# A decoder layer on one core: large raw tiles for the MLP's chained weights, one copy per value tile, and a later place for two steps of the attention's end

## The chip, the cores and the metric

The kernel runs on one core of a Trainium2 chip. The time is device microseconds of one execution; what counts is the median over runs.

## The reference, cut to what matters

One layer of a hybrid decoder over 512 tokens of width 1024, all in float32:

```
h = RMSNorm(x);  z = h @ W_in            # 1024 x 9728: retention q,k,v,gate; three attention groups q,k,v; two merge gates
A = retention(q, k, v), four heads, group RMSNorm, times swish(gate)
B = three groups of dilated causal window attention, (window, dilation) = (128,1), (512,4), (2048,16),
    QK-norm and rotary, the groups merged by their softmax denominators
x = x + W_o( sig(g_A) * (A @ W_A) + sig(g_B) * (B @ W_B) )
x = x + W_down( relu(RMSNorm(x) @ W_up)^2 )          # 4096 wide
x = x + sig(RMSNorm(x) @ W_pg) * (p @ W_pp)
```

## The kernel before, in words

**Matmuls in three parts.** Each float32 operand is split into a high part (rounded to the fast format, ACT, L250) and a low part (what is left, DVE, L251); a product is three matmuls, high x high, high x low, low x high (`mm3`, L262 to L264).

**Seven products instead of eight.** Most large products are done by `seven_products` (L1249): a 2 x 2 block scheme with seven products 1 to 7, each of two halves over the contraction. Its weights are seven blocks: B11, B21, B22 as they are, and T1 to T4, which are sums. A *unit* is half of such a block, 256 x 512 numbers. `SEVEN` and `HALVES` (L34, L37) are two orders of the products: `SEVEN` begins with halves (1,0), (5,0), (1,1), (5,1), `HALVES` with (1,0), (1,1), (5,0), (5,1); the rest is the same. Product 1 uses B11 and product 5 uses T1, so the units' order at the start is B11.0, T1.0, B11.1, T1.1 in `SEVEN` and B11.0, B11.1, T1.0, T1.1 in `HALVES`.

**The plan of weights.** `make_plan` (L1457) lists all units in the order of use; `plan_seven` (L171) makes the units of one seven. T2 grows out of T1's raw tile, T3 out of B22's and T4 out of T2's: when a unit is split, an accumulating DMA on the POOL queue adds another block onto the same raw tile (L228). So T1's and B22's raw tiles stay in use until the split of T4 and T3. A block named in `vector` gets its sum on DVE instead (L226, T1 += B11, T4 = T2 + B21): `self.added` says behind which unit's split it is put into the program.

**Buffers.** Raw tiles come from a ring of 6 (`wraw`, L87; 4 KB in each partition), the split ones from rings of 4, activations from 16 large buffers of 8 KB (`bigp`, L89): in the MLP seven for the normed input, two for the residual, up to seven for the inner activation `U`. `fetch` (L199) puts loads on SP's queue (L212); `ahead` (L217) splits units up to 2 ahead of their use.

**Order of the work.** `later` (L110) hangs a step on a clock that ticks with every half product of one side (6 matmuls); `tick` (L122) releases due steps. Three stretches, among them the first projection and the last down product, keep the program's order on ACT and DVE (`manual_schedule`); elsewhere the framework's scheduler orders each engine's instructions.

**Around the change.** `attention` (L699) does the projections of the three groups, their scores and values. `values_seven` (L732) makes the values of a group as a seven and, for the second half of its output, writes each of four value tiles in dilated order, token 4l + q to row l, place q: four DMAs each, one per q (L763, L764), on SP. `scores` (L771) hangs a block's softmax on the clock, and `turn` (L802) hangs the transposes of its exponentials on PE (L694) 5, 8 or 11 ticks behind it, by group. For the last group, `rescale` (L856) first merges the denominators (L863 to L878), scales the exponentials on ACT (L876) and transposes the merged factors on PE (L884). Behind it come the projection for the rotated queries (`ret_cols`, L992), and `retention` (L1013) with two pairs of heads, each with a seven for values and gates (L1045, planned at L1468). The MLP in `tail` (L1408) has four rounds of an up and a down product, 256 columns a matmul in up and 512 in down, planned at L1474 and L1475. The seven of the last group's values is called S2 below.

Of the kernel before, what the change touches and what calls it, by code (L numbers as in the profile page):

```python
# [11 lines left out]
F32 = mybir.dt.float32  # L12
# [5 lines left out]
P = 128  # L18
# [9 lines left out]
DIL = 4  # L28
# [51 lines left out]
class Block:  # L80


    def __init__(self, ctx, tc, a):
# [18 lines left out]
        self.hook = None  # L102
        self.chained, self.added = {}, {}
        self.spare = False
        self.plan, self.raws, self.loaded, self.used = [], [], [], 0
# [64 lines left out]

    def plan_seven(self, w, r0, c1, c2, order, vector=()):  # L171

# [5 lines left out]
        for name, u in units:  # L178
            if name == "T1":
                src = q(0, 1, u) if name in vector else (q(0, 1, u), q(0, 0, u))  # L180
                if name in vector:
                    self.added[at("B11", u)] = at("T1", u), at("B11", u)
            elif name == "T4" and name in vector:
                self.added[max(at("B21", u), at("T2", u))] = at("T2", u), at("B21", u)
                src = (None, at("T2", u))
            elif name[0] == "B":
                src = q(int(name[1]) - 1, int(name[2]) - 1, u)
            else:
                prev, ij = {"T2": ("T1", (1, 1)), "T3": ("B22", (0, 1)), "T4": ("T2", (1, 0))}[name]
                k = at(prev, u)  # L190
                self.chained[k] = q(*ij, u)
                src = (None, k)
            self.plan.append((src, None))

# [4 lines left out]
    def fetch(self, n):  # L199
        while len(self.raws) < min(len(self.plan), n):  # L200
# [4 lines left out]
            if src is None:  # L205
                self.raws.append((self.raws[add[0]][0], None))
                continue
            raw = self.wraw.tile([P, 1024], F32, tag="raw", name=self.nm("raw"))
            k = src.shape[0] // P
# [522 lines left out]
    def values_seven(self, scale, ready=None):  # L732
# [11 lines left out]
        def after(m, p, ps):  # L744
# [17 lines left out]
            if m in (6, 7):  # L762
                for q in range(DIL):  # L763
                    nc.sync.dma_start(tile(1)[32 * t : 32 * (t + 1), q], o[q : P : DIL])  # L764
            if m in (2, 4) and ready is not None:
# [5 lines left out]
    def scores(self, g, qT, kT, rq, past, held=None, lag=2):  # L771
# [7 lines left out]
        def block(r):  # L779
# [19 lines left out]
            for e in es:  # L799
                self.later((5, 8, 11)[g], lambda e=e: turn(e, r), ("pT", g, r))  # L800

# [211 lines left out]
    def retention(self, dec, kd):  # L1013
# [8 lines left out]
        for pr in range(2):  # L1022
# [21 lines left out]

            self.seven_products(left, after)  # L1045
            A.append(self.big("A"))
# [410 lines left out]
    def make_plan(self):  # L1457
# [9 lines left out]
        for c in (0, 512):  # L1467
            self.plan_seven(w, 0, RV + c, RG + c, SEVEN, ("T1", "T4"))  # L1468
        self.plan_mix()
# [3 lines left out]
        for f in range(NF // 2):  # L1473
            self.plan_seven(a["w_up"][0], 0, 1024 * f + 512, 1024 * f, HALVES, ("T1",))  # L1474
            self.plan_seven(a["w_down"][0], 1024 * f, 512, 0, HALVES, ("T1",))  # L1475
        for half in range(2):
# [40 lines left out]
```

## Time and profile before

| | |
|---|---|
| median of 3 runs | 952.26 us (951.79 to 953.13) |
| the profiled execution's own time | 955.36 us |
| its span, first to last instruction | 953.6 us |
| mean granted TensorE clock | 0.997 |
| share of the span: PE, DVE, ACT, POOL | 99%, 75%, 59%, 17% |
| MLP, four rounds | 585 to 895 us of the span |

PE is the matmul engine; PEld its loading of the stationary operand, which overlaps; DVE, ACT, POOL and SP are the vector, scalar, GpSimd and sync engines, and a q behind a name is an engine's queue of instructions. The granted clock is the share of full speed that the matmul engine gets. A wait in brackets is the idle time of the engine just before the instruction, with what ended it; where several things were waited for, the profile names the last. Matmul records overlap: at full clock, one of 512 columns starts every 0.23 us, though its record is 0.39 us long.

### The profile page before, as it was taken

Reading aid. Unit: us, or ns where it says so; the run is one execution under the profiler, and the core shown is the slowest. Engines: PE = TensorE matmul, PEld = TensorE weight load, DVE = VectorE, ACT = ScalarE, POOL = GpSimd, SP = SyncE. Lnnn points to the kernel's source line nnn. Section 1 sums busy time; section 2 is a strip of 40 time slices with the busy share of each in tenths; the row PEclk is TensorE's granted clock in tenths of the full one; section 3 lists DMA queues with packets and bytes.
Section 4 is the critical chain, followed back from the end, with each engine's and each line's share of the span. In section 5 each row is a group of like instructions: output and inputs, shape, how many; then the busy total and the mean of one; then the engine's idle time right before and its main releaser. Section 6 shows DMA issues by size and latency. Waiting matters only on the chain.

```text
span 953.6 us, 14325 instructions
## 1 busy us (share of the span) xinstructions
PE 943.3 (99%) x5357; PEld 826.2 (87%) x5357; DVE 718.4 (75%) x997; ACT 562.1 (59%) x1065; POOL 159.5 (17%) x140
## 2 busy tenths in 40 slices
PE   9999999999899999999999999999999999999998
PEld 6888888888788888999988888988998998998887
DVE  7789964766697849386937889799499689769953
ACT  5657775445745566576714446884494486467651
POOL 0322210222001112223012211111212302112100
PEclk9999999999999999999999999999999999999999
DMA  9953466258437645869737677868958968876911
GB/s 333 282 170 82 106 141 215 64 118 195 148 111 155 173 100 138 163 181 217 232 115 236 148 178 214 206 153 222 199 156 202 191 183 157 224 172 159 288 50 56
DMA packets 92549, 162.87 MB, mean 171 GB/s; under 512 B 8608, under 2 KB 20544, under 8 KB 92480
## 3 DMA queue, kind: packets, MB, share of 16 engines
q1 hardware_dynamic: 65168, 113.37, 36.4%
q0 software_dynamic: 23936, 46.14, 29.0%
q10 hardware_dynamic: 3376, 2.44, 0.9%
q8 instruction: 42, 0.69, 0.3%
q14 instruction: 27, 0.22, 0.1%
HBM read 153.49 MB, written 6.34 MB: 168 GB/s over the span
## 4 chain that ended last, share of the span: by engine, by line
PE 92%; DVE 3%; ACT 1%; issue 1%; DMA 1%; POOL 1%; SPq 0%; ACTq 0%; POOLq 0%; DVEq 0%
PE pg L264 25%; PE pg L262 25%; PE pg L263 25%; PE pa L264 3%; PE pa L263 3%; PE pa L262 3%; PE po L835 1%; PE ph L590 1%; DVE wlo L251 1%; PE pe L694 1%; PE sc L787 1%; PE ry L1083 1%; PE kv L1070 1%; PE ry L1085 1%; DVE ro L578 0%
## 5 line engine op out<-in xcount | busy, mean ns | idle before, releaser
L251 DVE TENSOR_TENSOR wlo<-raw,whi 128x1024 fp32r<-128x1024 f32 (+1 forms) x258 | 306.8, 1198 | 112.7 <-ACT whi L250 111.8
L250 ACT ACTIVATE whi<-raw 128x1024 fp32r<-128x1024 f32 (+1 forms) x257 | 266.3, 1041 | 212.1 <-PE pg L264 87.2
L263 PE MATMUL pg<-f,whi 128*128 128x256 f32 x384 | 108.7, 283 | 0.0
L264 PE MATMUL pg<-f,wlo 128*128 128x256 f32 x384 | 108.7, 283 | 0.0
L262 PE MATMUL pg<-f,whi 128*128 128x256 f32 x384 | 108.7, 283 | 0.0
L262 PE MATMUL pg<-whi,hh 128*128 128x512 f32 x248 | 98.6, 398 | 0.0
L264 PE MATMUL pg<-whi,hl 128*128 128x512 f32 x248 | 97.1, 392 | 0.0
L263 PE MATMUL pg<-wlo,hh 128*128 128x512 f32 x248 | 96.8, 390 | 0.0
L262 PE MATMUL pg<-whi,f 128*128 128x512 f32 x192 | 75.4, 393 | 0.0
L263 PE MATMUL pg<-wlo,f 128*128 128x512 f32 x192 | 74.8, 389 | 0.0
L264 PE MATMUL pg<-whi,f 128*128 128x512 f32 x192 | 74.8, 389 | 0.0
L262 PEld LDWEIGHTS pg<-f,whi 128*128 128x128 f32 x384 | 73.7, 192 | 0.2
L263 PEld LDWEIGHTS pg<-f,whi 128*128 128x128 f32 x384 | 73.7, 192 | 0.2
L264 PEld LDWEIGHTS pg<-f,wlo 128*128 128x128 f32 x384 | 73.7, 192 | 0.0
L228 POOL DMA_DIRECT2D raw<-in_w_in x32 | 38.9, 1216 | 197.8 <-DVE wlo L251 193.0
L264 PEld LDWEIGHTS pg<-whi,hl 128*128 128x128 f32 x248 | 46.6, 188 | 9.8
L263 PEld LDWEIGHTS pg<-wlo,hh 128*128 128x128 f32 x248 | 46.6, 188 | 9.2
L262 PEld LDWEIGHTS pg<-whi,hh 128*128 128x128 f32 x248 | 46.6, 188 | 9.2
L228 POOL DMA_DIRECT2D raw<-in_w_down x24 | 29.0, 1215 | 139.3 <-DVE wlo L251 108.2
L262 PE MATMUL pg<-whi,us 128*128 128x512 f32 x128 | 52.1, 407 | 0.0
L228 POOL DMA_DIRECT2D raw<-in_w_up x24 | 29.0, 1211 | 135.0 <-DVE wlo L251 124.7
L264 PE MATMUL pg<-whi,us 128*128 128x512 f32 x128 | 50.0, 391 | 0.0
(280 smaller groups left out, 2298.0 us busy)
## 6 DMA issues: line engine op xcount, KB each, us to landing
raw<-in_w_in SPq DMA_DIRECT2D x72, 512.0 KB, 4.1
raw<-in_w_in POOLq DMA_DIRECT2D x32, 512.0 KB, 6.2
raw<-in_w_up SPq DMA_DIRECT2D x32, 512.0 KB, 4.6
raw<-in_w_down SPq DMA_DIRECT2D x32, 512.0 KB, 4.6
raw<-in_w_up POOLq DMA_DIRECT2D x24, 512.0 KB, 6.6
raw<-in_w_down POOLq DMA_DIRECT2D x24, 512.0 KB, 5.9
x<-in_x SPq DMA_DIRECT2D x8, 512.0 KB, 8.2
raw<-in_w_ret_out SPq DMA_DIRECT2D x8, 512.0 KB, 3.8
```

The costliest lines, as they stand in the source:

```text
L228: self.nc.gpsimd.dma_start(raw, self.chained[i].rearrange("(k p) n -> p k n", p=P), accum_op=ALU.add)
L250: self.pin(nc.scalar.activation(R(hi[:, i]), raw[:, i], AF.Copy))
L251: nc.vector.tensor_tensor(R(lo[:, i]), raw[:, i], hi[:, i], op=ALU.subtract)
L262: t.matmul(ps, sh, mh, start=first, stop=False, skip_group_check=more)
L263: t.matmul(ps, sh, ml, start=False, stop=False, skip_group_check=more)
L264: t.matmul(ps, sl, mh, start=False, stop=last, skip_group_check=more)
L590: self.nc.tensor.transpose(ps[:, t * P : (t + 1) * P], rots[t][:, h * HD : (h + 1) * HD], self.ident)
L694: self.nc.tensor.transpose(ps[:, k * P : (k + 1) * P], e[:, k * P : (k + 1) * P], self.ident)
L787: nc.tensor.matmul(sc[:, h * P : (h + 1) * P], qT[:, h, rs], kT[:, h, rs], start=True, stop=True)
L835: nc.tensor.matmul(po[:, h * P : (h + 1) * P], v[:, vt, h * HD : (h + 1) * HD], pt, start=b == 0, stop=b == len(blocks) - 1)
L1070: nc.tensor.matmul(ps, kd[:, n, hs], v[:, n, c], start=True, stop=True)
L1083: nc.tensor.matmul(y, sT[0][:, r], v[:, i, c], start=True, stop=i == 0)
```

## The change

Four edits:

- T1's and B22's raw tiles of the MLP's products come from the large buffers, one for both halves.
- A value tile is written in dilated order by one DMA.
- The retention's two sevens are planned and run in `HALVES`, and where T4 is summed on DVE too, the sum T1 += B11 is put one unit later into the program: half 0 behind the split of B11.1, half 1 behind the split of T1.0.
- The last group's exponentials are transposed 15 ticks behind their softmax instead of 11.

```diff
-    def plan_seven(self, w, r0, c1, c2, order, vector=()):
+    def plan_seven(self, w, r0, c1, c2, order, vector=(), wide=()):
...
                 if name in vector:
-                    self.added[at("B11", u)] = at("T1", u), at("B11", u)
+                    self.added[at("B11", u) if "T4" not in vector else at("T1", u) - 1] = at("T1", u), at("B11", u)
...
+            if name in wide:
+                self.wide[len(self.plan)] = at(name, 0), u
             self.plan.append((src, None))
...
     def fetch(self, n):
...
-            raw = self.wraw.tile([P, 1024], F32, tag="raw", name=self.nm("raw"))
+            if len(self.raws) in self.wide:
+                n, u = self.wide[len(self.raws)]
+                if n not in self.pairs:
+                    self.pairs[n] = self.big("raw")
+                raw = self.pairs[n][:, 2 * u : 2 * u + 2].rearrange("p a b -> p (a b)")
+            else:
+                raw = self.wraw.tile([P, 1024], F32, tag="raw", name=self.nm("raw"))
...
             if m in (6, 7):
-                for q in range(DIL):
-                    nc.sync.dma_start(tile(1)[32 * t : 32 * (t + 1), q], o[q : P : DIL])
+                nc.sync.dma_start(tile(1)[32 * t : 32 * (t + 1)], o)
...
-                self.later((5, 8, 11)[g], lambda e=e: turn(e, r), ("pT", g, r))
+                self.later((5, 8, 15)[g], lambda e=e: turn(e, r), ("pT", g, r))
...
-            self.seven_products(left, after)
+            self.seven_products(left, after, HALVES)
...
-            self.plan_seven(w, 0, RV + c, RG + c, SEVEN, ("T1", "T4"))
+            self.plan_seven(w, 0, RV + c, RG + c, HALVES, ("T1", "T4"))
...
-            self.plan_seven(a["w_up"][0], 0, 1024 * f + 512, 1024 * f, HALVES, ("T1",))
-            self.plan_seven(a["w_down"][0], 1024 * f, 512, 0, HALVES, ("T1",))
+            self.plan_seven(a["w_up"][0], 0, 1024 * f + 512, 1024 * f, HALVES, ("T1",), ("T1", "B22"))
+            self.plan_seven(a["w_down"][0], 1024 * f, 512, 0, HALVES, ("T1",), ("T1", "B22"))
```

More of the change, by code (lines that the diff above doesn't have):

```diff
@@ L103, in __init__ @@
         self.chained, self.added = {}, {}
+        self.wide, self.pairs = {}, {}
         self.spare = False
```

## The prediction, made before the change was run

> **What bounds the kernel now.** I read the page first, then the waits of TensorE, then the timeline around the one long wait, then tables by stretch.
>
> ```profile
> span 953.6 us, 14325 instructions
> PE 943.3 (99%) x5357; PEld 826.2 (87%) x5357; DVE 718.4 (75%) x997; ACT 562.1 (59%) x1065; POOL 159.5 (17%) x140
> ```
>
> TensorE is busy for 943.3 of 953.6 us, and the change neither adds nor removes a matmul. So nothing is to be won but the 10.3 us in which PE waits, and what hides in slow matmuls. The waits of PE alone (who waited for whom: us in total, times, longest) are a short list:
>
> ```profile
> PE pc L884 <- DVE wide L878: 3.0, 1, 3.0
> PE warm L439 <- DVE warm L435: 1.4, 1, 1.4
> PE sc L795 <- DVE sm L678: 0.8, 1, 0.8
> PE pg L493 <- ACT hh L473: 0.3, 1, 0.3
> PE pg L262 <- ACT pp L533: 0.2, 1, 0.2
> ```
>
> Two of the five lie at the start (L439, L493), one in the first attention group (L795), one in the embedding (L533); the diff touches none of them. One is left: the transpose at L884 in `rescale(2)`, which waits 3.0 us for `wide`. The timeline of all engines (start, us, engine, line, what; idle before it in brackets) shows why:
>
> ```profile
> 247.70 1.23 DVE L251 TENSOR_TENSOR wlo<-raw,whi 128x1024 fp32r<-128x1024 f32 x1 [0.27 <-ACT whi L250]
> ...
> 249.64 1.22 DVE L251 TENSOR_TENSOR wlo<-raw,whi 128x1024 fp32r<-128x1024 f32 x1
> ...
> 251.69 0.20 ACT L864 ACTIVATE f<-f 128x16 f32<-128x16 f32 x1
> ...
> 252.48 0.39 PE L262 MATMUL pg<-whi,hh 128*128 128x512 f32 x1
> 252.70 0.39 PE L263 MATMUL pg<-wlo,hh 128*128 128x512 f32 x1
> 253.73 1.22 DVE L226 TENSOR_TENSOR raw<-raw,raw 128x1024 f32<-128x1024 f32 x1 [2.79 <-DMA v<-m]
> 254.22 1.04 SPq L212 DMA_DIRECT2D raw<-in_w_in  x2
> 254.88 0.17 DVE L866 TENSOR_TENSOR w<-f,st 128x16 f32<-128x16 f32 x1
> ...
> 255.63 4.79 ACT L876 ACTIVATE se<-se,inv 128x128 f32<-128x128 f32 x16 [2.86 <-DVE inv L870]
> 255.78 0.18 DVE L878 COPY wide<-f 128x16 f32<-128x16 f32 x1
> 256.11 0.37 PE L884 MATMUL pc<-ident,wide 128*16 128x128 f32 x1 [3.02 <-DVE wide L878]
> 256.13 0.78 PE L264 MATMUL pg<-whi,hl 128*128 128x512 f32 x1
> 256.71 0.63 PE L694 MATMUL pe<-ident,se 128*128 128x128 f32 x2
> ```
>
> The small steps that make `wide` (L866 to L878) could start when ACT is done with L864, at 251.69 + 0.20 = 251.89. But ahead of them in DVE's queue stands L226, the sum T1 += B11 for the first retention pair, which waits 2.79 us for a transfer. The profile names the value copies; the queue says which transfer it was:
>
> ```profile
> 244.40 1.58 SPq L212 DMA_DIRECT2D raw<-in_w_in  x2
> 246.87 7.26 SPq L764 DMA_DIRECT2D v<-m  x8
> ```
>
> The second of the two loads started at 245.6 us. Asked for line L212 in the stretch 245.5 to 246.0, the trace gives its time to landing:
>
> ```profile
> DMA to landing us min/median/max: 8.0/8.0/8.0
> ```
>
> For all L212 loads of the program the same row reads:
>
> ```profile
> DMA to landing us min/median/max: 3.3/4.4/10.9
> ```
>
> 245.6 + 8.0 = 253.6, and the sum starts at 253.73. So a weight load that took 8.0 instead of 4.4 us held DVE, DVE held `wide`, and `wide` held PE. The wait has a tail (columns: PE, PEld, DVE, ACT, POOL busy, then granted clock, DMA share, GB/s):
>
> ```profile
> 105.00:110.00 5.00, 4.17 (x20) 3.25 (x19) 5.00 (x8) 2.25 (x6) 1.24 (x1) 1.00 0.16 15
> ...
> 256.00:258.00 2.00, 1.89 (x8) 1.56 (x8) 0.00 (x0) 2.00 (x9) 0.00 (x0) 0.50 0.93 352
> 258.00:260.00 2.00, 2.00 (x10) 1.53 (x10) 0.00 (x0) 2.00 (x8) 0.00 (x0) 0.67 0.35 135
> 260.00:265.00 5.00, 5.00 (x27) 4.15 (x26) 4.26 (x8) 4.88 (x13) 0.00 (x0) 1.00 0.27 87
> ```
>
> After the 3.02 us the granted clock is 0.50 for 2 us and 0.67 for 2 us: 2 x 0.50 + 2 x 0.33 = 1.66 us more. The shorter wait of 0.8 us near 108 left it at 1.00. The whole place costs 3.02 + 1.66 = 4.7 us.
>
> **The change, part by part.** *Sums a unit later, product one's halves first.* The order of the pair becomes B11.0, B11.1, T1.0, T1.1 instead of B11.0, T1.0, B11.1, T1.1. The load that started at 244.40 stays B11.0, but the one at 245.6 becomes B11.1, on which no early sum depends. T1.0 is now the third load, one of the pair that went out at 254.22. The two splits at 247.70 and 249.64 free raw buffers at 248.9 and 250.9, so it can go out at about 249 at the earliest and lands at 249 + 4.4 = 253.4 by the median. If the sum then stands behind the small steps, these run from 251.89 to 251.89 + (255.78 + 0.18 - 254.88) = 252.97, and L884, which followed `wide` by 0.15 us, goes at 253.12. PE would reach it 0.23 us (252.48 to 252.70) after its last matmul, at 252.93. Of 3.02 us 0.2 is left, and the low clock goes: 4.5 us gained. What is late next there is ACT: its 16 scalings (4.79 us) then run from about 252.4 to 257.2, beside matmuls.
>
> *Last exponentials later.* The 16 transposes of `e` (L694) stand right behind L884 on PE, and each needs one of the 16 scalings. Unmoved and without the wait, they would begin near 253.5 and wait for ACT until about 257: up to 3.5 us given back. Four ticks are 4 x 6 matmuls x 0.23 = 5.5 us, so they come at about 259, after the scalings. The cover is the rotation's projection (`ret_cols`), whose matmuls need none of this. The reader behind them is the weighing with the values, at 269.93 before; it slips by some us, and PE has the projection to go on with. I cost it at nothing; without the cover it is those 3.5 us.
>
> ```profile
> 269.93 0.89 PE po L835 x8
> ```
>
> ```profile
> L764 SPq DMA_DIRECT2D v<-m x32: 467/586/1614, 133.6 to 253.7; - x32
> ```
>
> *One copy per value tile.* 32 issues on SP at 0.586 us become 8: 14 us of SP's time, none of it on PE's path. The bytes are the same. What it brings is that the loads behind it go out as their buffers come free, near 249 and 251, not at 254.22. It did not hold the 8.0 us load, which was issued before the eight copies. The Trainium skill, page "DMA: Bandwidth & Descriptors", section "Issuing engines are not separate DMA queues", says that all queues end on the same 16 engines and that spreading issues saves only the time to issue; by it this edit alone would leave the wait of 3.02 us where it is, and the sum by it would be 952.26.
>
> *MLP weights in large tiles.* The T1 and B22 units of the MLP move from the ring of 6 raw buffers, which they hold through their chains, to the 16 large buffers. No transfer, sum or split is added; loads of the next B11 and B21 can go earlier. What stalls are there to remove?
>
> ```profile
> 665.00:705.00 40.00, 40.00 (x333) 39.92 (x333) 26.00 (x28) 26.07 (x37) 7.25 (x6) 1.00 0.77 182
> 705.00:744.00 39.00, 39.00 (x176) 32.01 (x175) 37.55 (x48) 22.40 (x29) 7.25 (x6) 1.00 0.82 192
> ```
>
> ```profile
> 738.04 0.39 PE L264 MATMUL pg<-whi,f 128*128 128x512 f32 x1
> 738.30 0.47 PE L262 MATMUL pg<-whi,f 128*128 128x512 f32 x1
> ```
>
> PE never idles in these stages. Its starts slip by some 0.1 us (738.04 to 738.30 instead of 0.23). I bound the gain by 0 and 0.6 us over the four rounds and take 0.2; the loss is the second rival.
>
> **The sum.** In the profiled run, 955.36 us (span 953.6 and 1.8 around it): 4.5 + 0.2 = 4.7 us. That run is 3.1 us above the median of 952.26, and a part of this may be the very wait, since a load of 8.0 us is not the usual one. The gain on the median lies between 4.7 - 3.1 = 1.6 and 4.7; I take 4.2, near the upper end, because PE is otherwise full and little else is there for the profiler to lengthen: 952.26 - 4.2, rounded to 948.0. The forecast's own range is 946.6 to 950.7.
>
> **Rivals.** *The wait stays, somewhat shorter.* Outside the stretches ordered by hand the scheduler of the framework places L226, and it put it ahead of steps that come earlier in the program. If it does so again, the sum starts at 253.4, L866 follows 1.15 us later (253.73 to 254.88), `wide` is 1.08 us behind that and L884 another 0.15: 255.8, which is 2.9 us late; with the shortest landing, 3.3 us, 1.8 late. That gains 0.1 to 1.2 us, and 1.7 more if the clock stays up. For it speaks that the old place was filled the same way; against it, that T1.0 now comes two loads later than the gap which it filled. 949.4 to 952.2, say 951.2. The Trainium skill, page "TensorE: Matmul & The Clock Gate", section "Part 1: The HAM clock gate", has the clock halve after an idle window of about 3.4 us whose phase runs freely. By that rule a wait of 1.8 us would mostly keep the full clock and this rival would end at its fast end; the trace has 0.8 us without and 3.02 us with the loss, and nothing between.
>
> *Large buffers run short, and DVE waits in the MLP: slower.* In a down stage DVE is busy 37.55 of 39 us, so 1.45 us of idling is all it can afford. The large buffers hold seven activation tiles (`h2`), two of the residual and up to seven of `U`; that is all 16 without the raw tiles. If the next round's T1 tile gets its buffer only from the last round's, it is free when T4's split ends:
>
> ```profile
> 736.26 1.23 DVE L251 TENSOR_TENSOR wlo<-raw,whi 128x1024 fp32r<-128x1024 f32 x1 [1.20 <-ACT whi L250]
> 737.41 0.74 DVE L1286 SCALAR_TENSOR_TENSOR x<-pg,f,x 128x512 f32<-128x512 f32 x1
> 738.07 1.21 DVE L226 TENSOR_TENSOR raw<-raw,raw 128x1024 f32<-128x1024 f32 x1
> ```
>
> At 737.5 + 4.4 = 741.9 it lands; the sum, at 738.07 in DVE's queue, makes DVE wait 3.8 us, and the reads of PSUM behind it (L1286), for which PE waits, come 3.8 - 1.45 = 2.4 us late. Three such passages give 7 us, with landings of 8.0 us 18. 948 + 7 = 955, up to 966; I put it at 956. It decides from where the buffer comes free later than 738.07 - 4.4 = 733.7. Against it: `U`'s tiles go one by one, as their products end, and the sum need not keep its place.
>
> **How the numbers follow.** 0.2% is 1.9 us, about what a measurement of this kernel can tell from no change: faster is below 950.4, slower above 954.2. Forecast 0.60 (0.57 of it faster, 0.03 same), the wait stays 0.22 (0.05 faster, 0.17 same), buffers run short 0.18 (0.17 slower, 0.01 same). Together: faster 0.62, same 0.21, slower 0.17. The range goes from the forecast's low end, 946.6, to 953.0, over the wait that stays; it leaves out nearly all of the slow case.
>
> **What would show it.** Right: in the waits of PE the line for L884 is gone or under 0.5 us; the stretch after S2 has clock 1.00; L226 stands behind L878 on DVE; L764 has 8 issues; the transposes L694 of the last group lie some 5 us behind L884, without idle before them. Wrong: L226 still ahead of L866 with an idle time of over 1 us; or, in the MLP stages, DVE idle ahead of L226 and PE below its stretch; or a new line of over 1 us in PE's waits anywhere between 130 and 470 us.

## The result and the profile after

The change makes the kernel slower: 957.63 us (956.87 to 958.9) against 952.23 us for the kernel before, a ratio of 1.0057 (95% interval 1.0039 to 1.0074). The forecast was 948.0 with a range to 953.0. The profiled execution of the kernel after took 958.9 us, with a span of 957.1. One disturbed execution of the kernel before, 1575.79 us, is left out of everything below.

Lines of the kernel after are 8 or 9 higher than those of before in the parts that matter: the raw load L212 is L221, the sum L226 is L235, the accumulate L228 is L237, the split on ACT and DVE L250 and L251 are L259 and L260, the matmuls L262 to L264 are L271 to L273, the read of PSUM into the residual L1286 is L1294, the transpose L884 is L892.

The waits of PE in the kernel after (us in total, times, longest):

```profile
PE pg L271 <- DVE x L1294: 3.3, 3, 1.8
PE warm L448 <- DVE warm L444: 1.4, 1, 1.4
PE pg L273 <- DVE wlo L260: 1.1, 2, 0.6
PE sc L803 <- DVE sm L687: 0.9, 1, 0.9
PE pa L272 <- DVE wlo L260: 0.7, 1, 0.7
PE pg L502 <- ACT hh L482: 0.3, 1, 0.3
PE pg L272 <- DVE wlo L260: 0.3, 1, 0.3
```

The line of 3.0 us at the transpose is gone. In its place there are waits behind L1294 and the splits, none of which was in the list of before, and all of them lie in the MLP. The timeline around the transpose of the kernel after shows the small steps of `rescale(2)` running straight through, with no sum among them:

```profile
252.93 0.18 DVE L879 TENSOR_TENSOR f<-f,inv 128x16 f32<-128x16 f32 x1
252.99 4.80 ACT L884 ACTIVATE se<-se,inv 128x128 f32<-128x128 f32 x16
253.14 0.18 DVE L886 COPY wide<-f 128x16 f32<-128x16 f32 x1
253.44 0.09 PEld L892 LDWEIGHTS pc<-ident,wide 128*16 128x16 f32 x1 [0.47 <-PE pg L272]
253.47 0.27 PE L892 MATMUL pc<-ident,wide 128*16 128x128 f32 x1
...
257.11 1.23 DVE L235 TENSOR_TENSOR raw<-raw,raw 128x1024 f32<-128x1024 f32 x1 [3.79 <-DMA raw<-in_w_in]
```

The sum stands behind them now and waits 3.79 us for its load, and no wait of PE follows from it. The stretches behind the transpose keep the clock (PE, PEld, DVE, ACT, POOL, granted clock, DMA share, GB/s):

```profile
253.00:257.00 4.00, 3.92 (x18) 2.96 (x17) 0.29 (x2) 4.00 (x15) 0.00 (x0) 1.00 1.01 245
257.00:262.00 5.00, 5.00 (x28) 4.21 (x27) 4.89 (x8) 4.88 (x13) 0.00 (x0) 1.00 0.23 77
```

So the wait went, and the MLP lost more than that. The first matmul of the MLP (the 3094th) starts at 582.85 us instead of 586.87. But in a second profile of the kernel before (further down) it starts at 582.71: against that execution the attention gained nothing. Where one of the new waits comes from is seen in the second round's down stage. Four rows, ACT's, DVE's and PE's timelines of the kernel after:

```profile
737.04 2.16 ACT L259 ACTIVATE whi<-raw 128x1024 fp32r<-128x1024 f32 x2 [3.54 <-DMA raw<-in_w_down]
```

```profile
738.13 1.23 DVE L260 TENSOR_TENSOR wlo<-raw,whi 128x1024 fp32r<-128x1024 f32 x1 [1.59 <-ACT whi L259]
739.27 0.75 DVE L1294 SCALAR_TENSOR_TENSOR x<-pg,f,x 128x512 f32<-128x512 f32 x1
```

```profile
740.16 0.47 PE L271 MATMUL pg<-whi,f 128*128 128x512 f32 x1 [0.71 <-DVE x L1294]
```

ACT sits idle for 3.54 us until a transfer of `w_down` lands. That is the accumulate that makes T4's second half. Its split on DVE comes at 738.13, the read of PSUM (the memory that matmuls write) stands behind the split, at 739.27, and PE waits 0.71 us for the bank that it empties. Over the MLP (585 to 900 us) ACT's waits for such transfers have doubled; first the row of before, then the rows of after:

```profile
ACT whi L250 <- DMA raw<-in_w_down: 9.2, 5, 3.0
```

```profile
ACT whi L259 <- DMA raw<-in_w_down: 18.5, 7, 3.5
ACT whi L259 <- DMA raw<-in_w_up: 5.0, 4, 2.1
```

To compare stages between kernels I count matmuls. All kernels here run 5357, in the same order in the MLP, so the 3958th stands at the same place of the second round's down stage everywhere (712.09 us in the kernel after). I call it the marked matmul, and give times from its start; the 250 matmuls from it on take 45.35 us when nothing waits. Counted so over all eight stages, the kernel after loses 7.2 us against the same kernel without large weight tiles (first experiment): 2.0 in the first up stage, 3.05, 0.9 and 1.05 in the down stages of the first three rounds, 0.2 in the fourth round as a whole, and nothing in the other two up stages.

### The profile page after: what moved, and what is told of

Its sections match the earlier page's. It is cut to its first block, busy times and chain, and to the rows that moved or that the text cites. A ratio compares the mean times of both kernels' runs of the same rounds, so it can differ in the third digit from the quotient of the medians.

```text
span 957.1 us, 14255 instructions
## 1 busy us (share of the span) xinstructions
PE 944.2 (99%) x5357; PEld 825.2 (86%) x5357; DVE 719.4 (75%) x997; ACT 561.3 (59%) x1065; POOL 159.6 (17%) x140
## 4 chain that ended last, share of the span: by engine, by line
PE 77%; DMA 8%; issue 5%; DVE 5%; ACT 2%; POOL 2%; SPq 0%; ACTq 0%; POOLq 0%; DVEq 0%
PE pg L271 21%; PE pg L273 21%; PE pg L272 21%; DMA raw<-in_w_down 5%; PE pa L273 2%; PE pa L272 2%; PE pa L271 2%; DMA raw<-in_w_up 2%; PE po L843 1%; POOL raw L237 1%; DVE wlo L260 1%; PE ph L599 1%; ACT whi L259 1%; PE sc L795 1%; PE ry L1091 1%
## 5 line engine op out<-in xcount | busy, mean ns | idle before, releaser
L260 DVE TENSOR_TENSOR wlo<-raw,whi 128x1024 fp32r<-128x1024 f32 (+1 forms) x258 | 306.8, 1200 | 116.9 <-ACT whi L259 115.6
L259 ACT ACTIVATE whi<-raw 128x1024 fp32r<-128x1024 f32 (+1 forms) x257 | 265.8, 1041 | 218.6 <-PE pg L273 80.6
L273 PE MATMUL pg<-f,wlo 128*128 128x256 f32 x384 | 108.7, 284 | 1.1 <-DVE wlo L260 1.1
L271 PE MATMUL pg<-f,whi 128*128 128x256 f32 x384 | 108.7, 283 | 0.1
L271 PE MATMUL pg<-whi,hh 128*128 128x512 f32 x248 | 98.8, 398 | 0.0
L273 PE MATMUL pg<-whi,hl 128*128 128x512 f32 x248 | 96.9, 391 | 0.0
L271 PE MATMUL pg<-whi,f 128*128 128x512 f32 x192 | 75.3, 393 | 3.3 <-DVE x L1294 3.3
L273 PEld LDWEIGHTS pg<-f,wlo 128*128 128x128 f32 x384 | 73.6, 192 | 1.5 <-DVE wlo L260 1.5
L273 PE MATMUL pg<-whi,f 128*128 128x512 f32 x192 | 74.8, 390 | 0.0
L271 PEld LDWEIGHTS pg<-f,whi 128*128 128x128 f32 x384 | 73.7, 192 | 0.5 <-ACT whi L259 0.3
L237 POOL DMA_DIRECT2D raw<-in_w_in x32 | 38.9, 1216 | 192.4 <-DVE wlo L260 187.5
L273 PEld LDWEIGHTS pg<-whi,hl 128*128 128x128 f32 x248 | 46.5, 188 | 9.8
L271 PEld LDWEIGHTS pg<-whi,hh 128*128 128x128 f32 x248 | 46.6, 188 | 9.4 <-ACT whi L259 0.2
L237 POOL DMA_DIRECT2D raw<-in_w_down x24 | 29.1, 1220 | 142.5 <-DVE wlo L260 113.4
L237 POOL DMA_DIRECT2D raw<-in_w_up x24 | 29.0, 1219 | 139.1 <-DVE wlo L260 138.9
L271 PE MATMUL pg<-whi,us 128*128 128x512 f32 x128 | 52.0, 407 | 0.0
L272 PE MATMUL pg<-wlo,us 128*128 128x512 f32 x128 | 50.1, 391 | 0.0
```

Of the source, the lines that this page charges most:

```text
L237: self.nc.gpsimd.dma_start(raw, self.chained[i].rearrange("(k p) n -> p k n", p=P), accum_op=ALU.add)
L259: self.pin(nc.scalar.activation(R(hi[:, i]), raw[:, i], AF.Copy))
L260: nc.vector.tensor_tensor(R(lo[:, i]), raw[:, i], hi[:, i], op=ALU.subtract)
L271: t.matmul(ps, sh, mh, start=first, stop=False, skip_group_check=more)
L272: t.matmul(ps, sh, ml, start=False, stop=False, skip_group_check=more)
L273: t.matmul(ps, sl, mh, start=False, stop=last, skip_group_check=more)
```

## Experiments

### The large tiles, and which of them

The first kernel is the one after with the weights of the MLP back in the ring:

```diff
-            self.plan_seven(a["w_up"][0], 0, 1024 * f + 512, 1024 * f, HALVES, ("T1",), ("T1", "B22"))
-            self.plan_seven(a["w_down"][0], 1024 * f, 512, 0, HALVES, ("T1",), ("T1", "B22"))
+            self.plan_seven(a["w_up"][0], 0, 1024 * f + 512, 1024 * f, HALVES, ("T1",))
+            self.plan_seven(a["w_down"][0], 1024 * f, 512, 0, HALVES, ("T1",))
```

> All of the change but the large tiles. Theory A (the large tiles alone made the MLP slower, by about 7 us of matmul waits in the profile; the other three edits gained what was forecast): 947.5 to 950.6 us, no wait of PE over 0.5 us after 590 us. Theory C (the loss comes from the retention's new order, which shifts everything behind it): 956 to 958, the waits in the MLP stay.

Measured: 951.75 us, ratio to the kernel before 0.9988 (0.9975 to 1.0001). Theory C is out. Theory A is right on where the loss is, but the time lies above its range: the other three edits gain less than was forecast. The second kernel is the one before with the large tiles alone (the same two lines, the other way).

> The kernel before with the large tiles alone. Theory A: 952.2 + 7 = about 959 us, waits of PE of 0.5 to 2 us at the end of each down stage, and the 3.0 us at the transpose of wide as before. Theory C: 952.

Measured: 958.35 us, ratio 1.0060 (1.0040 to 1.0080). The large tiles cost it all, 0.6% alone or with the rest. The profile of this second kernel holds a second finding. Its attention is that of the kernel before, and yet the wait at the transpose (here L893) is not 3.0 us but 0.2:

```profile
PE pc L893 <- DVE wide L887: 0.2, 1, 0.2
```

More on this below. Then one half of the edit at a time, in the kernel after, in the up and the down line alike: only T1 in large tiles, then only B22.

```diff
-HALVES, ("T1",), ("T1", "B22"))
+HALVES, ("T1",), ("T1",))
```

> The change, with T1 alone in large tiles, B22 back in the ring. Theory A in its form 'sixteen large buffers are too few for two more tiles': one tile fewer frees the room, most of the loss goes, 949 to 953. Theory B (the rival of the prediction: the sum T1 += B11 stands in DVE's queue and waits for T1's late load): the loss stays whole, 956 to 958.

Measured: 955.95 us, ratio 1.0032 (1.0015 to 1.0048), in neither range but next to B's. B's mechanism is hardly there: in the MLP the sums wait 0.9 us for loads in all. The first up stage runs as without large tiles; the down stages still lose.

```diff
-HALVES, ("T1",), ("T1", "B22"))
+HALVES, ("T1",), ("B22",))
```

> The change, with B22 alone in large tiles, T1 back in the ring. Theory A: as for T1 alone, most of the loss goes, 949 to 953. Theory B: all of the loss goes, 948 to 950.6, since no sum waits for B22.

Measured: 975.79 us, ratio 1.0236 (1.0217 to 1.0256). Neither theory had this: half of the edit costs four times the whole. The waits of DVE and of PE in the MLP say by what:

```profile
DVE raw L235 <- DMA raw<-in_w_down: 37.7, 8, 6.6
```

```profile
PE pg L271 <- DVE r L1333: 13.8, 6, 3.3
```

The sum T1 += B11 stands at the head of DVE's queue for 37.7 us, waiting for loads, and reads of PSUM (L1333) behind it come late. This is the rival that the prediction priced at 956, in another kernel than the one it was priced for.

### Up or down, and one more buffer

Theory A was now: loads into large tiles wait until matmuls let a large buffer go, then bunch beside the accumulating transfers, which land late. Three kernels test it, and a fourth tests the waiting sum.

```diff
-            self.plan_seven(a["w_down"][0], 1024 * f, 512, 0, HALVES, ("T1",), ("T1", "B22"))
+            self.plan_seven(a["w_down"][0], 1024 * f, 512, 0, HALVES, ("T1",))
```

> After with large tiles for w_up's T1 and B22 only; w_down's units are back in the six-slot ring. Theory A (a large raw tile can be loaded only when product matmuls let a large buffer go, so the next up's loads bunch beside the last accumulating transfers of the down stage, whose units land late): the losses of the down stages of rounds 0 to 2, 4.8 us over those of before (3.05, 0.7, 1.06), stay to more than half, since it is the up's loads that collide there, and the median is 953.5 to 957. Rival B (the loss belongs to the stage whose own units lie in halves of a large tile: their accumulates or splits are slower): the down stages run as before, at most 1 us of the 4.8 is left, the 2.0 us of the first up stage stays, and the median is 952 to 954.

Measured: 972.14 us, ratio 1.0199 (1.0174 to 1.0223), far outside both. The down stages, whose own tiles are in the ring, lose most, so rival B is out; and A had the size wrong. PE's waits in the MLP:

```profile
PE pg L271 <- DVE x L1294: 9.7, 3, 4.6
```

SP's and POOL's timelines in the second round's down stage (start, us until the last issue ends, count):

```profile
719.88 1.92 SPq L221 DMA_DIRECT2D raw<-in_w_up  x4
```

```profile
722.15 1.20 POOL L237 DMA_DIRECT2D raw<-in_w_down  x1 [5.63 <-ACT whi L259]
725.21 1.20 POOL L237 DMA_DIRECT2D raw<-in_w_down  x1 [1.85 <-DVE wlo L260]
727.31 2.49 POOL L237 DMA_DIRECT2D raw<-in_w_down  x2 [0.90 <-DVE wlo L260]
```

Four loads of the next up stage go out within 2 us, just ahead of four accumulates. The accumulates land 10.8, 11.2, 13.0 and 15.8 us after their issue. Without large tiles the same four take 5.9, 6.0, 6.4 and 10.1.

```diff
-            self.plan_seven(a["w_up"][0], 0, 1024 * f + 512, 1024 * f, HALVES, ("T1",), ("T1", "B22"))
+            self.plan_seven(a["w_up"][0], 0, 1024 * f + 512, 1024 * f, HALVES, ("T1",))
```

> After with large tiles for w_down's T1 and B22 only; w_up's units are back in the ring. Theory A: no load for an up stage waits for a large buffer, so the down stages' last accumulates are alone or nearly so; the down stages of rounds 0 to 2 lose at most 1.5 us of the 4.8, the first up stage at most 0.5 of 2.0, and the median is 951 to 953.5. Rival B: the down stages lose 4 us or more as in the kernel after, and the median is 955 to 957.

Measured: 955.78 us, ratio 1.0024 (1.0013 to 1.0035). The first up stage loses 0.3 us, the down stages of rounds 0 to 2 lose 1.6, 1.1 and 1.4: less than in the kernel after, more than A said. Time and losses (4.1 us together) lie where B put them. B alone is out by the run before, where the down stages lose most with no large tile of their own; but a stage's own large tiles do cost it something. Here it is the stage's own B22 that goes out as a pair, at 704.56 and 705.03, just ahead of the two accumulates that make T2 (706.13 and 707.27); these land after 8.3 and 9.7 us instead of 5.9 and 5.9.

```diff
-        self.bigp = pool("bigp", 16)
-        self.tmpp = pool("tmpp", 12)
+        self.bigp = pool("bigp", 17)
+        self.tmpp = pool("tmpp", 8)
```

> After with 17 large buffers in place of 16, paid with 8 small work tiles in place of 12, which also changes the order of a stretch of the attention; so the MLP stages are compared, stage by stage, at the same matmuls. Theory A: one of the two large raw tiles no longer waits for the products; the losses of the down stages of rounds 0 to 2 fall from 4.8 us to 2.4 or less, and SP's waits for product reads (31.0 us in 10) to under a half. Rival B: the losses stay within 1 us of 4.8, whatever the number of buffers. The whole time, by A: 952 to 955.5, if the attention costs nothing.

Measured: 967.61 us, ratio 1.0143 (1.0122 to 1.0165), part of it in the attention. In the MLP, where A expected half of the loss or less, it is larger; PE's waits there:

```profile
PE pg L271 <- DVE x L1294: 6.6, 3, 2.7
```

That is 6.6 us against 3.3 in the kernel after, and the down stages of rounds 0 to 2 lose 8.4 us against 5.0, so B's "within 1 us" is out too. The seventeenth buffer let two more loads of the next up stage out at 719.7 and 720.2, ahead of the four accumulates. The part of A that says "too few large buffers" has fallen: the loads were not too late, they were too early.

The fourth is the kernel with only B22 in large tiles, with eight slots in the ring instead of six.

```diff
-        self.wraw = pool("wraw", 6)
+        self.wraw = pool("wraw", 8)
...
-        self.tmpp = pool("tmpp", 12)
+        self.tmpp = pool("tmpp", 8)
```

> After with only B22 in large tiles (975.79 us, 18 us over the kernel after) and a ring of eight slots in place of six, paid with 8 small work tiles in place of 12. Theory C (T1's long chains hold slots of the ring, B11's load comes late, and its sum stands at the head of DVE's queue, DVE 37.7 us for eight loads, with the reads of PSUM behind it): with two more slots B11 loads in time, DVE waits under 10 us for loads, and the time is 952 to 962. Rival D (the planner's order of DVE is what is bad, whatever the slots): DVE still waits 25 us or more and the time stays over 968.

Measured: 970.79 us in one execution. DVE's waits for `w_down` in the MLP are gone from the top of its list and those for `w_up` are 1.7 us, as C said and against D. The time lies above C's range and in D's, but not for D's reason: the attention now loses time that it didn't with six slots (a matmul of the first up stage, the 3165th, starts at 600.4 us instead of 591.8).

### Holding the loads back

If loads go out too early, a gate should help. Each load into a large tile is made to wait for a write of one element per partition that stands in DVE's order:

```diff
                 raw = self.pairs[n][:, 2 * u : 2 * u + 2].rearrange("p a b -> p (a b)")
+                self.tc.keep_in_program_order(self.nc.vector.memset(raw[:, :1], 0.0))
...
-            self.fetch(i + 1)
+            self.fetch(i + 1 + (4 if self.wide and i + 4 > min(self.wide) else 0))
```

> After with each load into a large tile held back by a write of one element per partition that stands in DVE's order (32 small instructions), the loads planned four units earlier; the loads go one at a time instead of as soon as a buffer is there. Theory A' (with more large buffers the losses grew, so it isn't that loads wait for buffers: loads that nothing meters go out in groups of two to five beside the accumulating transfers and stretch them): the accumulates of the down stages land in 5.5 to 7 us, the last in 10, the down stages lose at most 2.5 us against 5.2 in the kernel after (both over the same kernel without large tiles), and the median is 951 to 954.5. Rival E (a load into a large tile comes too late for its split as it is): held back further it comes later still, the losses grow, and the median is 958 or more.

Measured: 961.83 us, ratio 1.0086 (1.0068 to 1.0103). Both theories were half right: the accumulates of the second round's down stage land as A' said, the time is E's. The waits behind L1294 are gone, and others have come; the head of PE's list in the MLP:

```profile
PE pg L272 <- ACT whi L260: 5.8, 5, 2.6
```

In the second round's down stage T4's second half now lands 8.5 us after its issue, the quickest of all kernels, and PE doesn't wait for it. But B22, held back by the gate, is loaded only at 715.74 us, 2.3 us after the marked matmul, and ACT and PE wait for it:

```profile
721.01 2.00 ACT L260 ACTIVATE whi<-raw 128x1024 fp32r<-128x1024 f32 x2 [2.65 <-DMA raw<-in_w_down]
```

```profile
723.07 0.73 PE L272 MATMUL pg<-whi,f 128*128 128x512 f32 x2 [1.09 <-ACT whi L260]
```

With the loads planned two units earlier instead of four:

> As the run with four units, but the loads are planned two units earlier only. Theory A': the accumulates land as quickly, but T1's load now comes so shortly before its sum that DVE waits for it at the head of its queue, some 1 to 2 us in each of the eight stages; time 954 to 965. Rival E: later still than with four units, over 965.

Measured: 997.29 us in one execution, in rival E's range: loads that come too late cost much more. Between too early and too late the gate found no good place here.

### A longer ring, and loads that nobody reads

The next two take the kernel before with the second edit (the sums a unit later), without any large weight tile, with eight small work tiles; the second of them has eight slots in the ring.

```diff
-        self.tmpp = pool("tmpp", 12)
+        self.tmpp = pool("tmpp", 8)
```

> The kernel before with the second edit and 8 small work tiles in place of 12: the control for the next run. By either theory the MLP stages run as with the second edit alone (second half of T4 landing 21 to 24 us after the marked matmul of a down stage, no loss there); the attention may cost some us, since its order changes. 951 to 962.

Measured: 952.88 us, ratio 0.9991 (0.9982 to 1.0000), as expected.

```diff
-        self.wraw = pool("wraw", 6)
+        self.wraw = pool("wraw", 8)
```

> As the control, with a ring of eight slots for raw weights in place of six, and no large tile anywhere. Theory A' (six slots meter the loads; whatever lets them go sooner puts them beside the accumulates): loads go out up to two slots sooner, the second half of T4 lands 1 us or more later in the down stages, and the MLP stages lose 2 us or more against the control, most of it ahead of T4. Rival F (it is the large tiles themselves, loaded in pairs 0.4 us apart and queued on SP behind loads for the ring; a longer ring of single tiles does no harm): MLP stages within 0.5 us of the control, T4's landings within 0.5 us.

Measured: 976.61 us, ratio 1.0239 (1.0224 to 1.0255). Two more slots cost 24 us, and by neither theory's way. T4's second half lands as in the control (in the first down stage 23.2 us after the corresponding matmul, the 3454th, against 23.7), so F's reading of the transfers holds and A' fails there. The loss lies in the late part of the up stages and in the attention. DVE's and PE's waits in the MLP with eight slots:

```profile
DVE raw L235 <- DMA raw<-in_w_down: 34.8, 8, 6.1
```

```profile
PE pg L271 <- DVE r L1334: 10.6, 5, 2.8
```

And DVE's timeline at the end of the first up stage, with eight slots and then with six:

```profile
618.60 1.22 DVE L235 TENSOR_TENSOR raw<-raw,raw 128x1024 f32<-128x1024 f32 x1 [5.15 <-DMA raw<-in_w_down]
...
621.18 1.28 DVE L1334 TENSOR_TENSOR r<-r,pg 128x512 f32<-128x512 f32 x2
```

```profile
609.32 1.28 DVE L1334 TENSOR_TENSOR r<-r,pg 128x512 f32<-128x512 f32 x2
...
613.75 1.23 DVE L235 TENSOR_TENSOR raw<-raw,raw 128x1024 f32<-128x1024 f32 x1 [1.19 <-DMA raw<-in_w_down]
```

With eight slots the sum has moved ahead of the pair of PSUM reads (L1334) and waits 5.15 us for its load; with six it stands behind them and waits 1.19. The framework's scheduler sets the order on DVE when the kernel is built. That it pulls the sum forward because more slots free the load earlier in its reckoning is argued; the traces show only that the order changed, and what it cost.

The last pair asks whether loads beside T4's accumulates alone make these land late. In the first three down stages two extra loads go out that nobody reads; the two kernels differ only in their size. (The lines that say which accumulates have such loads behind them are left out.)

```diff
+            if i in self.beside:
+                extra = self.big("extra")
+                self.tc.keep_in_program_order(self.nc.gpsimd.memset(extra[:, 0, :1], 0.0))
+                for h, src in enumerate(self.beside[i]):
+                    self.nc.sync.dma_start(extra[:, 2 * h : 2 * h + 2], src.rearrange("(k p) n -> p k n", p=P))
```

> The kernel before with the second edit, no large weight tile, and in each of the first three down stages two extra loads of 512 KB that nobody reads, into a free large buffer, released by a one-element write on POOL just behind T4's last accumulate. Theory A' (loads beside an accumulating transfer stretch it, and PE pays for each microsecond that T4's second half lands past 23.9 after the marked matmul): it lands 2 to 4 us later than in the second edit alone (21.3, 22.9, 23.1), the three stages lose 2 to 6 us together, the median is 953 to 957. Rival G (the accumulates of the kernel after are late because they start late, the bytes beside them don't matter): landings within 1 us, median 951 to 952.5.

Measured: 951.44 us, ratio 0.9987 (0.9974 to 1.0000).

> The control: the same extra instructions in the same order, but 16 KB a partition set in place of 512 KB (8 of each 512 columns). Both theories: T4's second half lands as with the second edit alone, within 1 us, and the median is 951 to 952.5; if it is slower like the run with the whole loads, it is the place in SP's or POOL's queue that costs, not the bytes.

Measured: 951.19 us, ratio 0.9981 (0.9973 to 0.9990). Rival G is right about this place. (It isn't everywhere: with large tiles in up only, the last accumulate starts no later than here, and lands after 15.8 us.) SP's timeline with the whole loads, second round:

```profile
722.71 0.37 SPq L223 DMA_DIRECT2D raw<-in_w_up  x1
723.17 0.68 SPq L244 DMA_DIRECT2D extra<-in_w_down  x1
```

The last accumulate was issued at 721.4 and its issue took POOL until about 722.7. Both loads come at or behind that, and it lands after 8.8 us, with small loads after 9.3. The load at 722.71 landed after 7.7 us, where one alone takes 3.5 to 3.7. The packets that moved from 722.7 to 725.4 (queue, packets, MB, share of the 16 DMA engines) all belong to the accumulates' queue:

```profile
q0 software_dynamic: 285, 0.55, 113.0%
```

So a load that is issued behind accumulates waits at first, and does no harm. The kernel with large tiles in up only has the opposite order, four loads ahead of an accumulate that is issued at 722.15. There, from 723 to 727, nearly all packets are the loads':

```profile
q1 hardware_dynamic: 658, 1.27, 100.4%
q0 software_dynamic: 1, 0.00, 0.0%
```

In the first experiment, with one load ahead of it in place of four, the same accumulate moves 235 packets in the stretch that lies as far behind its issue.

The other extra load of each stage wasn't held by the write and went out 2.5 to 3.5 us ahead of T2's two accumulates; only in the second round did these land later than with the small load, by 1.3 and 2.2 us.

### The other three edits, and the wait at the transpose

> The kernel before, unchanged, for a second profile. If the late load (8.0 us to land) and the 3.02 us wait of the first transpose belong to the kernel, they are here again, with a span within 1 us of 953.6. If they were one execution's, the load lands in 4 to 6 us, the wait is under 0.5 us and the span is 949 to 951.

Measured: 951.35 us, span 949.6. The kernel before, unchanged, in a second profile:

```profile
PE warm L439 <- DVE warm L435: 1.4, 1, 1.4
PE sc L795 <- DVE sm L678: 0.7, 1, 0.7
PE pc L884 <- DVE wide L878: 0.7, 1, 0.7
```

0.7 us instead of 3.0. The load that took 8.0 us to land takes 5.7 here. The second edit alone:

```diff
-                    self.added[at("B11", u)] = at("T1", u), at("B11", u)
+                    self.added[at("B11", u) if "T4" not in vector else at("T1", u) - 1] = at("T1", u), at("B11", u)
...
-            self.seven_products(left, after)
+            self.seven_products(left, after, HALVES)
...
-            self.plan_seven(w, 0, RV + c, RG + c, SEVEN, ("T1", "T4"))
+            self.plan_seven(w, 0, RV + c, RG + c, HALVES, ("T1", "T4"))
```

> The kernel before with the second edit only (product one's halves first in the retention pairs, the sum a unit later). If the wait of 3.02 us at the first transpose and the low clock after it are there in most executions of the kernel before, this alone is 3 to 4.7 us faster: 948 to 950 beside 952.5 to 953.3. If they were an accident of one load in the profiled execution, it is 951 to 953, and the wait is under 0.5 us in its profile.

Measured: 951.44 us, ratio 0.9975 (0.9963 to 0.9988), 1.8 us between the medians. It is faster than both kernels of the case. The copy alone, and the lag alone:

```diff
-                for q in range(DIL):
-                    nc.sync.dma_start(tile(1)[32 * t : 32 * (t + 1), q], o[q : P : DIL])
+                nc.sync.dma_start(tile(1)[32 * t : 32 * (t + 1)], o)
```

> The kernel before with the one copy per value tile alone. The prediction took nothing for it on PE's path: 951.5 to 953.5, ratio within 0.1% of 1. If SP's freed time matters (loads of the attention go sooner), 950 to 951.5; if the one large transfer holds others up, over 954.

Measured: 955.15 us, ratio 1.0016 (1.0004 to 1.0029).

```diff
-                self.later((5, 8, 11)[g], lambda e=e: turn(e, r), ("pT", g, r))
+                self.later((5, 8, 15)[g], lambda e=e: turn(e, r), ("pT", g, r))
```

> The kernel before with the last exponentials four ticks later alone. The prediction took nothing for it: 951.5 to 953.5, ratio within 0.1% of 1. If the cover of 3.5 us is not there, PE waits at the four row sums, 0.5 us or more each, and the median is over 954.

Measured: 953.60 us, ratio 1.0007 (0.9996 to 1.0018): nothing, as expected. The copy alone is slightly slower. Its profiled execution has the long wait at the transpose again, and a low clock behind it; its waits of PE, then its stretches:

```profile
PE pc L892 <- DVE wide L886: 2.2, 1, 2.2
PE warm L448 <- DVE warm L444: 1.4, 1, 1.4
PE pg L271 <- DVE r L1333: 1.3, 1, 1.3
```

```profile
253.00:257.00 4.00, 1.76 (x11) 1.38 (x10) 1.99 (x6) 2.21 (x8) 0.00 (x0) 0.88 0.85 249
257.00:262.00 5.00, 5.00 (x24) 3.99 (x23) 2.09 (x4) 5.00 (x17) 0.00 (x0) 0.75 0.01 2
```

So the wait belongs to a kernel without the second edit, but its length is a matter of the execution: 3.0, 0.7, 0.2, 2.2 and 1.0 us in the five profiles of such kernels (before twice, large tiles alone, copy alone, lag alone). Over the timed executions of the kernel before, 16 of 101 have a mean granted clock of 0.998 or less, and their mean is 955.8 us against 953.0 for the other 85. With the second edit and no large tile there are none in 58 executions of five kernels that keep six slots. That these 16 are executions with a long wait is argued from the two profiles with a low clock there; the executions themselves weren't profiled.

What the length hangs on is shown. In these five profiles the load of T1's first half, the one that took 8.0 us in the prediction's profile, lands after 8.04, 5.69, 5.22, 7.26 and 6.03 us, and each time the transpose starts 2.47 us after the landing. So the wait is the landing time less 5.0 us. In the profiles with the second edit and six slots the load in that place lands after 5.7 to 8.7 us, and PE's wait at the transpose is 0.14 us or less.

The copy alone lies where the third branch of its expectation put it, over 954. The same load speaks for that branch too: among the profiles with six slots it lands after 5.7 to 8.7 us (median 6.8) in the ten with one copy per value tile, and after 5.2 to 8.0 us (median 5.8) in the eight with four. In a kernel without the second edit that would make the wait about 1 us longer. The ranges overlap, so this is likely rather than shown.

## Why the prediction was wrong

**The step that failed is the term for the large tiles.** The prediction said "I bound the gain by 0 and 0.6 us over the four rounds and take 0.2; the loss is the second rival". The edit costs 0.6%, some 5.7 us, alone (1.0060) or taken out of the kernel after (957.63 against 951.75). The bound below zero was left to a rival with a chance of 0.18, and the range stopped at 953.0. The reasoning "no transfer, sum or split is added; loads can go earlier" took earlier loads for harmless. Nor do the lines shown bear the 0.6: matmuls that start 0.26 us apart (738.04 to 738.30) instead of 0.23 slip by 0.03 us, not by "some 0.1".

**What the runs show in its place.** The six-slot ring spaced the loads. Freed from it they go out in pairs or fours, and DVE's and SP's orders change with them. Two ways of losing time were seen in the kernel after.

One is the landing of T4's second half. In the second round's down stage, with times from the marked matmul (my count from the traces):

| kernel | last accumulate, issue to landing | 250 matmuls | over 45.35 |
|---|---|---|---|
| second edit alone | 13.5 to 22.9 | 45.35 | 0 |
| extra loads, whole | 13.7 to 22.5 | 45.35 | 0 |
| before, second profile | 13.8 to 23.4 | 45.35 | 0 |
| before, first profile | 13.6 to 24.0 | 45.61 | 0.26 |
| large tiles alone | 13.9 to 24.5 | 45.99 | 0.64 |
| six slots, eight work tiles | 13.5 to 24.6 | 46.25 | 0.90 |
| after | 13.9 to 24.8 | 46.31 | 0.96 |
| only T1 large | 13.9 to 24.9 | 46.37 | 1.02 |
| large in down only | 14.9 to 25.2 | 46.49 | 1.14 |
| 17 large buffers | 13.9 to 26.8 | 48.27 | 2.92 |
| large in up only | 13.5 to 29.3 | 52.44 | 7.09 |

Up to 23.4 PE loses nothing; from about 24 on each microsecond of landing costs about one of PE. (The last row also holds a stretch at half clock behind a wait of 4.6 us, some 1.7 us of the loss.) The other rounds agree: in the kernel after T4's second half lands at 26.9 in the first and at 24.9 in the third, with 3.05 and 1.05 us lost. In its second profile before had 0.6 us to spare here, and the kernel after used it up. In the kernel after, the pair of the next round's loads went out at 13.8 and 14.2, within the issue of the last accumulate (13.9 to 15.2). Loads at the end of that issue or behind it do no harm (the extra loads), earlier ones in greater number do more (up only, 17 buffers). That it is the order of issue which counts is what all rows and the packets of the two queues fit; no pair of runs changed that order and nothing else. The control with six slots shows that a landing also scatters: 24.6 with the same issue times that gave 22.9. So the 24.8 of the kernel after in this round would prove little by itself. Its 26.9 in the first round does: there the kernels without large tiles have 22.9 to 23.8.

The other is SP's order. SP's timelines ahead of the first up stage, before and then after:

```profile
582.82 0.38 SPq L212 DMA_DIRECT2D raw<-in_w_up  x1
...
586.75 0.42 SPq L212 DMA_DIRECT2D raw<-in_w_up  x1
```

```profile
578.77 0.38 SPq L221 DMA_DIRECT2D raw<-in_w_down  x1
...
582.73 0.40 SPq L221 DMA_DIRECT2D raw<-in_w_down  x1
...
588.85 2.12 SPq L221 DMA_DIRECT2D raw<-in_w_up  x3
```

With slots free in the ring, loads for the down stage go out ahead of those for the up stage, and the up stage's B22 goes out at 589.3 and 589.8 instead of 582.8 and 586.8. The first of the accumulates behind it follows at 7.7 us after the 3165th matmul, which I take as this stage's mark, instead of 0.1, and the stage loses 2.0 us. It loses nothing where B22 of `w_up` is in the ring (only T1 large: 30.0 us for 250 matmuls, the same as without large tiles), and the seventeenth buffer changes little (31.7 against 32.0).

**The rival "Large buffers run short"** had the sign and the size (956, 955 to 966) and the wrong mechanism, so that its time came near is luck. In the kernel after the sums L235 have no idle ahead of them in the MLP, and one more buffer makes it worse. The waiting sum that it described is real in two other kernels, B22 alone and eight slots, whose MLP takes 25 and 15 us more than that of the kernels they are compared with.

**The wait at the transpose** was read rightly: load, sum, small steps and transpose hang together as the prediction said, and the second edit takes the wait away. The predicted start of the transpose was 253.12 with the clock at 1.00, and it came at 253.47 with 1.00. The last exponentials' transposes come at 259.3, with no wait, as forecast. What was off is its size in plain executions. The prediction gave 1.6 to 4.7 us on the median and took 4.2, "near the upper end". The second edit alone gives 1.8 us. The profiled execution was 3.1 us above the median, and that was this very wait, as the prediction had offered and then set aside: the second profile's span is 4.0 us shorter, 2.3 us of it less wait and 1.7 us the low clock that it doesn't have.

**The lag** costs nothing, as said. **The copy** was put at nothing too; alone it is slower by 0.16% (0.04 to 0.29%), and together with the second and fourth edits it leaves 0.9988 where the second alone has 0.9975 (the intervals overlap). Four of its twelve executions have the low clock, and the load that the transpose waits for tends to land later with it, so a longer wait at the transpose may be all of it. The prediction's "It did not hold the 8.0 us load" is thus doubtful: a copy issued behind the load may still delay its landing. The profile of the copy alone shows 2.2 us at the transpose, and 1.3 us at L1333 that no edit explains. This stays open.

## What to carry to other kernels

A small ring of buffers is also a meter: it spaces the loads, and it sets the order in which in-order queues meet their waits. Before giving loads more room, find the transfer that PE waits for last in each stage, count how many microseconds it has to spare, and ask which loads will now be issued ahead of it. And a wait found in one profiled execution that is some us above the median should be priced from a second profile of the same kernel before a forecast is built on it.

## What was not expected of the hardware

- Accumulating transfers of 512 KB for `w_down`, in kernels without large tiles, land after 5.5 to 7.6 us when the one before went out 1.7 to 4 us earlier, and after 8.7 to 11.0 as the last of a close pair (1.1 to 1.3 us apart). Behind four loads issued just ahead, the last took 15.8. Plain loads of the same size land after 3.5 to 3.7 us alone and about 1.3 us apart when bunched.
- A load issued behind accumulates starts late (no packet in 2.7 us, landing after 7.7 us), though it is in another queue, and an accumulate issued behind four loads likewise (issued at 722.15, one packet of its queue from 723 to 727). The Trainium skill, page "DMA: Bandwidth & Descriptors", section "Issuing engines are not separate DMA queues", says that transfers of all issuing engines run on the same 16 engines and interleave; the trace agrees that they share, but here the order of issue shows through.
- The granted clock fell to 0.50 for 3.4 us after waits of 3.02 us (from 255.9 us, before) and 2.2 us (from 256.1 us, copy alone; the 0.88 and 0.75 shown above are means of longer stretches). It stayed at 1.00 after 0.7 and 1.0 us, but also after 2.69 us (at 618.55, B22 alone) and 2.86 us (at 830.78, up only). With large tiles alone it fell at 599.6, after waits of 1.17 and 0.52 us close together. So the length of one wait doesn't decide it. The Trainium skill, page "TensorE: Matmul & The Clock Gate", section "Part 1: The HAM clock gate", names an idle window of about 3.4 us; here the fall came after shorter waits than that, and not after all of them.
